# A fourth Strassen pair in the first half of the cross output projection, and a later place in the program for the loads of the transposed memory

## The chip, the cores and the metric

The kernel runs on one core of a Trainium2 chip. The metric is the device time of one execution in microseconds (us); lower is better. Three runs of the kernel before gave 2434.51, 2434.72 and 2436.06 us, a median of 2434.72 us.

## What is computed

One layer of a streaming encoder on 256 tokens of width 2048: a SwiGLU feed-forward block, a mixer of two attentions with gates, a cross attention on 256 memory tokens, and a second SwiGLU block, each followed by a residual and a LayerNorm. The change touches the cross attention:

```python
def memory_cross_attention(h, mem, mem_ln_g, mem_ln_b, w_xq, w_xkv, w_xo):
    m = layer_norm(mem, mem_ln_g, mem_ln_b)
    q = (h @ w_xq).reshape(b, s, X_HEADS, X_HEAD_DIM)          # 4 heads of 512
    kv = (m @ w_xkv).reshape(b, m_len, 2, X_HEADS, X_HEAD_DIM)
    k, v = kv[:, :, 0], kv[:, :, 1]
    sc = jnp.einsum('bqhd,bkhd->bhqk', q, k).astype(jnp.float32) / math.sqrt(X_HEAD_DIM)
    p = jax.nn.softmax(sc, axis=-1).astype(v.dtype)
    o = jnp.einsum('bhqk,bkhd->bqhd', p, v).reshape(b, s, D_MODEL)
    return o @ w_xo                                              # 256x2048 by 2048x2048
...
h = layer_norm(ALPHA * h + xa, ln_x_g, ln_x_b)
```

## The kernel before

**Precision.** Each float32 matrix is split into a high plane `hi` (a cast to fp32r on ScalarE, ACT, line 264 for weights and 255 for activations) and a low plane `lo` (source minus high plane on VectorE, DVE, lines 267 and 256). A product takes three matmuls: hi by hi, hi by lo, lo by hi. TensorE (PE) accumulates them in PSUM.

**Pairs.** The weights of a projection arrive in blocks of 128 x 2048 floats (1 MB, line 193, through three buffers `raw`). One block holds a pair of k-tiles by 1024 columns, and its number is `c`. `pair_group` takes the blocks in an order, by default 0, 1, 2 and so on. A plain pair (`mm_pair`, line 311) is 24 matmuls of 512 columns: two k-tiles, two halves of the tokens, two halves of the columns, three passes. A Strassen pair (`mm_sums`, line 366; the dictionary `at` says which pairs) needs 21, seven products by three passes. Four of the seven products go to four extra banks `qs`, which `shared` (lines 679 to 684) adds to the result once, behind the last such pair. For its 21 matmuls a Strassen pair needs sums of its weights (`weight_sums`, DVE, lines 248 and 250), high and low planes of 1536 columns of the block and of 2048 columns of sums where a plain pair has 2048 columns, and four forms of its activations (`sum_forms`, DVE, lines 321 and 325, then a cast on ACT and a subtraction on DVE, lines 255 and 256). In the cross output the staged sums lie in block T3 and their planes in T0 and T1, one buffer each.

**Cross output.** `cross` ends in `all_items`: `out_pair` computes the first 1024 output columns from eight pairs of `w_xo`, three of them (2, 4, 6) Strassen pairs; `out_proj` computes the other 1024 columns with plain matmuls (line 298) from `w_xo_r`, and its last part is woven with the LayerNorm of the first token half (`ln_scale`, `ln_T`: statistics at line 390, aggregation at 395, scaling at 413 and 415, transposes on PE at 421, planes at 428, 430, 255 and 256). Woven between the pairs are `out(2)` and `out(3)`, the products of probabilities and values for heads 2 and 3 (line 1543 before, 1545 after), and the forms. Heads 0 to 3 lie in H4, H5, X2, X3; pair `c` reads head `c // 2`. Behind comes the second feed-forward block, whose first weights (`ffn_gate`) are loaded while the LayerNorm runs.

**Memory.** `mem_norm` normalizes the memory tokens during the mixer's output projection (`w_out`). Its `load` (lines 1336 to 1342) sends the memory rows (`mem`, two loads into T1 and T2) and the transposed memory (`memT`, two loads into T3 and H4) on POOL's queue. It is woven in ahead of the first block of `w_out`. The mixer's last values are turned by DMA transposes on SP's queue (line 850) meanwhile.

**Order.** Each engine runs its instructions in the order in which the scheduler of the tile framework put them when the program was built; a wait holds whatever stands behind it on that engine. Buffers are given out by name, so a load waits until the last reader of its block is done.

Of the kernel before, what the change touches and what calls it, by code (L numbers as in the profile page):

```python
# [21 lines left out]
KT = D // P  # L22
# [12 lines left out]
AT_YB = (2, 4, 6), (4, 6)  # L35
SUMS_XQ = {4: ("H5", 0), 6: ("H5", 1), 2: None}
SUMS_XV = {4: ("T3", 0), 6: ("T3", 1), 2: None}
SUMS_XO = {2: None, 4: ("H2", 0), 6: ("H2", 1)}

AT_XQ = (4, 6), (2, 4, 6)  # L40
AT_XV = (2, 4, 6), (4, 6)
SUM_HOME = ("X2", "X3"),
# [59 lines left out]
class Kernel:  # L102
# [513 lines left out]
            turn = None  # L616
            f0 += nf

    def out_pair(self, bank, src, g, nk, x, at, fx, scale, st, sums_in=SUM_HOME):

        nc, h = self.nc, self.h
        ps, qs = {}, {}

        def shared():
            for (tt, a), s in qs["add"].items():
                c = (2 * g + a) * 512
                hs = h[tt][:, c:c + 512]
                if scale:
                    nc.vector.scalar_tensor_tensor(hs, hs, ALPHA, s, ALU.mult, ALU.add)
                else:  # L630
                    nc.vector.tensor_tensor(hs, hs, s, ALU.add)

        def finish():
            for tt in range(2):
                for a in range(2):
                    self.finish(tt, 2 * g + a, ps[tt, a], scale and not at, st)
        self.pair_group(bank, src, 512, nk, x, at, fx, ps, qs, shared, sums_in)
        self.add(finish)

    def group_tile(self, j):  # L640
# [690 lines left out]
    def mem_norm(self):  # L1331

        nc, t = self.nc, self.t
        e = self.mem = {}

        def load():
            e["m"] = [self.block(f"T{1 + tt}", (P, D)) for tt in range(2)]
            e["raw"] = [self.block(g) for g in ("T3", "H4")]
            for j in range(2):
                nc.gpsimd.dma_start(e["m"][j], t["mem"][j])  # L1340
            for j in range(2):
                nc.gpsimd.dma_start(e["raw"][j], t["memT"][:, 8 * j:8 * j + 8, :])

        def stat(tt):
            def fn():
                if tt == 0:
                    e["diag"] = self.w2((P, 4, P))
                    e["ones"] = self.w1((P, P))
                    nc.gpsimd.memset(e["ones"], 1.0)
                st = self.ln_begin()  # L1350
                with self.tc.issue_after(self.last_lo.ins):
                    for n in range(4):
                        self.ln_piece(st, e["m"][tt], n)
                kept = self.chain
                mean, r, _ = self.ln_scale(st)
                self.chain = kept
                for k, v in enumerate((mean, r)):
                    nc.vector.tensor_scalar(e["diag"][:, 2 * k + tt, :], self.ident, v, None, ALU.mult)
                if tt:
                    e["mT"] = self.act(["H0", "H1", "H2", "H3"])  # L1360
            return fn

        def spread():

            ps = self.at_tile()
            with self.tc.issue_after(self.last_mm.ins):
                for j in range(4):
                    nc.tensor.matmul(ps[:, j * P:(j + 1) * P], e["ones"], e["diag"][:, j, :], start=True, stop=True)
            e["mr"] = self.w2((P, 2, 1, S))
            nc.scalar.copy(e["mr"].rearrange("p a o s -> p (a o s)"), ps)  # L1370

        def quarter(q):
            def fn():
                v = e["raw"][q // 2][:, q % 2 * 4:q % 2 * 4 + 4, :]
                for k, op in enumerate((ALU.subtract, ALU.mult)):
                    nc.vector.tensor_tensor(v, v, e["mr"][:, k].to_broadcast([P, 4, S]), op)
                for j in range(4):
                    kt = 4 * q + j
                    nc.scalar.activation(v[:, j, :], v[:, j, :], AF.Identity,
                                         bias=self.vec("mem_ln_b", kt), scale=self.vec("mem_ln_g", kt))  # L1380
                self.split(v, e["mT"].blk(0, 4 * q, 4), e["mT"].blk(1, 4 * q, 4))
            return fn

        return {0: [load], 4: [stat(0)], 7: [stat(1)], 9: [spread], 10: [quarter(0)], 11: [quarter(1)], 13: [quarter(2)], 14: [quarter(3)]}

    def turned_norm(self, ln, st, x):

# [45 lines left out]
    def cross(self, xT, st, norm, steps_out):  # L1433
        nc, t, e = self.nc, self.t, self.mem
        q, k, v, sc, pt, o, turned = {}, {}, {}, {}, {}, {}, {}
        fq, fv, fx = {}, {}, {}
        m, x = lambda: e["mT"], lambda: o["t"]
# [96 lines left out]
        def out(h):  # L1534
            def fn():
                if h == 0:
                    o["t"] = Act([])
                o["t"].blocks += self.act([HEADS[h]]).blocks
                for j in range(4):
                    ps = self.mm_tile() if h > 1 else self.at_tile()  # L1540
                    for kt in range(2):
                        for i, (a, b) in enumerate(PASSES):
                            nc.tensor.matmul(ps[:, :S], v[h][:, a, kt, j * P:(j + 1) * P],
                                             pt[h][b][:, kt * S:(kt + 1) * S],
                                             start=(kt + i == 0), stop=(kt == 1 and i == 2))
                    self.split(ps[:, :S], o["t"].at(0, 4 * h + j), o["t"].at(1, 4 * h + j))
            return fn

        form_q = lambda c: self.forms_step(fq, SUMS_XQ, c, xT)
        form_v = lambda c: self.forms_step(fv, SUMS_XV, c, m)  # L1550
        form = lambda c: self.forms_step(fx, SUMS_XO, c, x)
        gb = lambda i: lambda: self.gb_apply(1, self.h, (i,))
# [13 lines left out]
        scale, planes, nsend, njoin = norm  # L1566
# [11 lines left out]
                    7: [join(3)]}, 1)  # L1578

        def all_items():  # L1580
            self.out_pair(1, t["w_xo"][0], 0, KT, x, SUMS_XO, fx, True, st, (("T0", "T1"), "T3"))
            self.out_proj("w_xo_r", KT, x, True, st, steps_out, (
                ("T0", "T1", "early"), ("T2", "T3", "early"), ("H0", "H1", "early"), ("H2", "H3", "early")), 2)
        self.weave(self.collect(all_items), {1: [out(2), out(3), form(2)], 2: [form(4)], 4: [form(6)]}, prio=0)

    def final_steps(self, st):
        nc, t, h = self.nc, self.t, self.h
# [83 lines left out]
def _tok(w):  # L1671

    k, n = w.shape
    return w.reshape(k // P, P, n // 512, 512).transpose(2, 1, 0, 3).reshape(n // 512, P, k // P * 512)


def _pairs(u, g, n, turned):


    import numpy as np  # L1680
    k, c = u.shape
    w = np.stack([m.reshape(k // P, P, c // n, n) for m in (u, g)])
    for j in range(c // n):
        for i in turned[j]:
            w[:, 2 * i:2 * i + 2, :, j] = w[::-1, 2 * i:2 * i + 2, :, j].copy()
    return w.transpose(3, 2, 1, 0, 4).reshape(c // n, P, k // P * 2 * n)


def _halves(w):

    w = w.reshape(w.shape[0], -1, 2, 512)
    return [w[:, :, i].reshape(w.shape[0], -1) for i in (0, 1)]
# [6 lines left out]
def _layout(i):  # L1699
# [45 lines left out]
    w = a["w_xo"][0]  # L1745
    r["w_xo"] = _pairs(*_halves(w[:, :D // 2]), 512, [SUMS_XO])
    r["w_xo_r"] = _tok(w[:, D // 2:])
# [29 lines left out]
```

## Time and profile before

| | |
|---|---|
| median of three runs | 2434.72 us |
| profiled execution | 2432.88 us, of which its span 2431.0 us |
| PE busy | 2422.4 us, 11280 matmuls |
| DVE busy | 2131.3 us |
| ACT busy | 1553.1 us |
| POOL busy | 36.0 us |
| DMA | 516.21 MB, mean 212 GB/s |
| cross output, first half (`w_xo`) | from 1649.68 to 1697.34 us in the span |

Times in the profile are microseconds from the start of the span. Busy time is the share in which an engine had at least one instruction in flight. A matmul's busy time (about 390 ns for 512 columns) overlaps its neighbours', so a rate is read from the starts of rows that follow each other. The same holds for DVE and ACT, where an instruction starts some 90 ns before the one ahead of it ends. A row of the timeline merges equal instructions (xcount); a bracket at its end tells the idle time before it and what ended it.

### The profile page before, as it was taken

The page shows a single profiled execution, that of the slowest core. Times are in us where ns is not written, and L with a number is a line of the kernel's source. Part 1 is how long each engine was busy: PE and PEld are TensorE (multiplying, and loading weights), DVE is VectorE, ACT ScalarE, POOL GpSimd, SP SyncE. Part 2 cuts the span into 40 slices and gives each one's busy share as a digit, 9 for nine tenths or more (in the row PEclk, how much of TensorE's full clock was granted, in tenths as well). Part 3 has the DMA queues.
Part 4 walks back from the last instruction along what each step waited for, and adds up shares of the span by engine and source line. Part 5 has one row for each costly group of instructions (what it writes and reads, how often), then busy time and mean ns, then how long its engine had stood idle before and what let it go on. Part 6 is the DMA issues. An engine that isn't in the chain of part 4 may idle for free.

```text
span 2431.0 us, 29704 instructions
## 1 busy us (share of the span) xinstructions
PE 2422.4 (100%) x11280; PEld 2021.5 (83%) x11280; DVE 2131.3 (88%) x2437; ACT 1553.1 (64%) x2022; POOL 36.0 (1%) x81
## 2 busy tenths in 40 slices
PE   9999999999999999999999999999999999999999
PEld 8888888889888888888888888888888888888887
DVE  8999989899889998789788889879879999888997
ACT  6676745666555557878565787755666675556662
POOL 0000000000000001000000000000000000000000
PEclk9999999999999999999999999999999999999999
DMA  7766656667645657776577577655556766666665
GB/s 267 253 211 215 206 201 223 210 202 230 218 174 211 216 202 242 236 203 176 186 254 246 170 237 214 216 183 192 191 199 213 228 222 211 219 207 207 201 222 180
DMA packets 176416, 516.21 MB, mean 212 GB/s; under 512 B 111729, under 2 KB 112497, under 8 KB 121105
## 3 DMA queue, kind: packets, MB, share of 16 engines
q1 hardware_dynamic: 170816, 495.83, 61.5%
q0 software_dynamic: 4592, 17.30, 2.3%
q8 instruction: 88, 1.44, 0.2%
q10 hardware_dynamic: 864, 1.18, 0.1%
q14 instruction: 56, 0.45, 0.1%
HBM read 485.30 MB, written 2.10 MB: 200 GB/s over the span
## 4 chain that ended last, share of the span: by engine, by line
PE 89%; DVE 4%; ACT 3%; DMA 2%; issue 1%; SPq 0%; DVEq 0%; ACTq 0%
PE at L311 25%; PE mm L311 24%; PE at L366 11%; PE mm L366 11%; PE mm L298 10%; PE mm L277 4%; PE mm L279 2%; DVE lo L267 2%; ACT hi L264 2%; PE at L1034 1%; DMA raw<-w_xq 1%; DMA raw<-w_xk 0%; DMA raw<-w_xv 0%; PE at L1088 0%; ACT w L832 0%
## 5 line engine op out<-in xcount | busy, mean ns | idle before, releaser
L264 ACT CAST hi<-raw 128x1024 fp32r<-128x1024 f32 (+1 forms) x852 | 803.4, 980 | 440.4 <-PE at L311 130.5
L267 DVE TENSOR_TENSOR lo<-raw,hi 128x2048 fp32r<-128x2048 f32 (+1 forms) x427 | 902.2, 2115 | 136.1 <-ACT hi L264 129.1
L311 PE MATMUL mm<-hi,T 128*128 128x512 f32 (+1 forms) x1312 | 308.1, 384 | 0.5 <-ACT hi L255 0.4
L264 ACT CAST X<-H 128x1024 fp32r<-128x1024 f32 (+1 forms) x170 | 174.7, 1034 | 171.5 <-DVE H L248 117.5
L311 PEld LDWEIGHTS mm<-hi,T 128*128 128x128 f32 x1312 | 244.4, 188 | 46.8 <-ACT hi L255 0.9
L311 PE MATMUL at<-hi,T 128*128 128x512 f32 x1136 | 272.3, 390 | 0.0
L311 PEld LDWEIGHTS at<-hi,T 128*128 128x128 f32 x1136 | 213.3, 188 | 44.4
L267 DVE TENSOR_TENSOR X<-H,X 128x2048 fp32r<-128x2048 f32 (+1 forms) x85 | 191.5, 2253 | 62.1 <-ACT X L264 61.9
L311 PE MATMUL mm<-lo,T 128*128 128x512 f32 (+1 forms) x656 | 158.1, 383 | 0.0
L311 PE MATMUL at<-lo,T 128*128 128x512 f32 x568 | 141.0, 390 | 0.0
L311 PEld LDWEIGHTS mm<-lo,T 128*128 128x128 f32 x656 | 122.2, 188 | 22.4
L311 PE MATMUL at<-hi,H 128*128 128x512 f32 x560 | 133.4, 390 | 0.0
L311 PEld LDWEIGHTS at<-lo,T 128*128 128x128 f32 x568 | 106.7, 188 | 22.1
L311 PEld LDWEIGHTS at<-hi,H 128*128 128x128 f32 x560 | 105.0, 188 | 21.5
L250 DVE TENSOR_TENSOR H<-H,raw 128x512 f32<-128x512 f32 (+1 forms) x170 | 115.7, 681 | 2.4
L311 PE MATMUL mm<-hi,H 128*128 128x512 f32 x480 | 115.6, 392 | 0.4 <-DVE w L684 0.4
L311 PEld LDWEIGHTS mm<-hi,H 128*128 128x128 f32 x480 | 89.6, 188 | 19.5 <-DVE w L684 0.8
L248 DVE TENSOR_TENSOR H<-raw 128x1024 f32<-128x1024 f32 (+1 forms) x85 | 102.2, 1203 | 0.5 <-DMA raw<-w_gate 0.3
L366 PE MATMUL mm<-X,X 128*128 128x512 f32 x342 | 91.3, 392 | 0.0
L264 ACT CAST X<-raw 128x1024 fp32r<-128x1024 f32 (+1 forms) x54 | 55.4, 1035 | 48.7 <-DVE raw L250 38.7
L366 PE MATMUL at<-X,X 128*128 128x512 f32 (+1 forms) x315 | 82.7, 386 | 0.0
L854 ACT COPY w<-w 128x1024 uint16<-128x1024 uint16 (+1 forms) x60 | 75.6, 1273 | 1.5 <-DMA w<-w 1.4
(387 smaller groups left out, 4153.9 us busy)
## 6 DMA issues: line engine op xcount, KB each, us to landing
raw<-ffn_w_in SPq DMA_DIRECT2D x150, 1024.0 KB, 4.9
raw<-ffn_w_out SPq DMA_DIRECT2D x66, 1024.0 KB, 4.9
raw<-w_gate SPq DMA_DIRECT2D x32, 1024.0 KB, 4.7
raw<-ffn_w_out_r SPq DMA_DIRECT2D x16, 1024.0 KB, 5.0
raw<-w_qk SPq DMA_DIRECT2D x16, 1024.0 KB, 5.3
raw<-w_o_b SPq DMA_DIRECT2D x16, 1024.0 KB, 4.8
raw<-w_out SPq DMA_DIRECT2D x16, 1024.0 KB, 5.1
raw<-w_xk SPq DMA_DIRECT2D x16, 1024.0 KB, 5.3
```

The source lines that it names most:

```text
L248: self.nc.vector.tensor_tensor(two[0], two[1], raw[:, :m].unsqueeze(1).to_broadcast([P, 2, m]), ALU.add)
L250: self.nc.vector.tensor_tensor(t[:, a * m:a * m + m], t[:, b * m:b * m + m], raw[:, a * m:a * m + m], ALU.add)
L264: self.last_hi = self.nc.scalar.copy(hi[:, c:d], src[:, c:d])
L267: self.last_lo = self.nc.vector.tensor_tensor(lo[:, :n], src, hi[:, :n].bitcast(F32), ALU.subtract)
L277: self.nc.tensor.matmul(ps, hi[j], x.both(kt), start=(j == 0), stop=False)
L279: self.last_mm = self.nc.tensor.matmul(ps[:, :S], lo[j], x.at(0, kt), start=False, stop=(j == n - 1))
L298: self.last_mm = self.nc.tensor.matmul(ps, x.at(xi, kt)[:, tt * P:(tt + 1) * P], w[wi][:, j * 512 + c:j * 512 + c + m], start=(start and j ...
L311: self.last_mm = self.nc.tensor.matmul(ps[tt, g][:, :n], x.at(xi, kt)[:, tt * P:(tt + 1) * P], w[wi][:, c:c + n], start=first and j + wi + ...
L366: self.last_mm = self.nc.tensor.matmul(bank[:, :m], a[xi], v[wi][:, c * m:(c + 1) * m], start=own and first and wi + xi == 0, stop=own and ...
L854: self.nc.scalar.copy(self.words(u, n).rearrange("p (c k) -> p k c", k=2), self.words(s, n).rearrange("p (k c) -> p k c", k=2))
L1034: nc.tensor.matmul(ps[:, c0:c0 + nk], q[:, tt * P:(tt + 1) * P], k[:, :nk], start=(j == 0), stop=(j == len(parts) - 1))
```

## The change

Pair 0 joins pairs 2, 4 and 6 as a Strassen pair; its forms go to block F. The eight blocks are taken in the order 1, 0, 3, 2, 4, 5, 6, 7. A form step for pair 0 is woven in ahead of the first block. In `mem_norm`, the allocation of the two buffers for the transposed memory and its two loads move to an item of their own, five blocks of `w_out` later. The host lays the blocks of `w_xo` out by the same dictionary.

```diff
-SUMS_XO = {2: None, 4: ("H2", 0), 6: ("H2", 1)}
+SUMS_XO, ORDER_XO = {2: None, 4: ("H2", 0), 6: ("H2", 1), 0: ("F", 0)}, (1, 0, 3, 2, 4, 5, 6, 7)
...
-    def out_pair(self, bank, src, g, nk, x, at, fx, scale, st, sums_in=SUM_HOME):
+    def out_pair(self, bank, src, g, nk, x, at, fx, scale, st, sums_in=SUM_HOME, order=None):
...
-        self.pair_group(bank, src, 512, nk, x, at, fx, ps, qs, shared, sums_in)
+        self.pair_group(bank, src, 512, nk, x, at, fx, ps, qs, shared, sums_in, order)
...
             e["m"] = [self.block(f"T{1 + tt}", (P, D)) for tt in range(2)]
-            e["raw"] = [self.block(g) for g in ("T3", "H4")]
             for j in range(2):
                 nc.gpsimd.dma_start(e["m"][j], t["mem"][j])
+
+        def load_turned():
+            e["raw"] = [self.block(g) for g in ("T3", "H4")]
             for j in range(2):
                 nc.gpsimd.dma_start(e["raw"][j], t["memT"][:, 8 * j:8 * j + 8, :])
...
-        return {0: [load], 4: [stat(0)], 7: [stat(1)], 9: [spread], 10: [quarter(0)], 11: [quarter(1)], 13: [quarter(2)], 14: [quarter(3)]}
+        return {0: [load], 4: [stat(0)], 5: [load_turned], 7: [stat(1)], 9: [spread], 10: [quarter(0)], 11: [quarter(1)], 13: [quarter(2)], 14: [quarter(3)]}
...
-            self.out_pair(1, t["w_xo"][0], 0, KT, x, SUMS_XO, fx, True, st, (("T0", "T1"), "T3"))
+            self.out_pair(1, t["w_xo"][0], 0, KT, x, SUMS_XO, fx, True, st, (("T0", "T1"), "T3"), ORDER_XO)
...
-        self.weave(self.collect(all_items), {1: [out(2), out(3), form(2)], 2: [form(4)], 4: [form(6)]}, prio=0)
+        self.weave(self.collect(all_items), {0: [form(0)], 1: [out(2), out(3), form(2)], 2: [form(4)], 4: [form(6)]}, prio=0)
```

How the built programs differ: up to the middle of the last block of `w_xv` the two programs have the same instructions in the same order on every engine. On POOL and SP the order is the same throughout, and the loads of `mem` and `memT` on POOL wait for the same semaphores at the same counts. From there on PE, DVE and ACT differ at the cross output.

PE just behind `out(2)`, before: the second plain block (pair 1, `hi_13311`) follows, with `out(3)` (`X_2056`) in its gaps.

```order
L1543 MATMUL mm_13402<-X_2039_13209,T_2055_13322 128x256 x6
L311 MATMUL at_13336<-hi_13311,H_1973_12758 128x512 x2
L311 MATMUL at_13337<-hi_13311,H_1973_12758 128x512 x2
L311 MATMUL at_13338<-hi_13311,H_1973_12758 128x512 x2
L311 MATMUL at_13339<-hi_13311,H_1973_12758 128x512 x2
L311 MATMUL at_13336<-hi_13311,H_1973_12758 128x512 x2
L1543 MATMUL mm_13412<-X_2039_13209,X_2056_13329 128x256 x6
```

PE at the same place with the change. `hi_13315` and `lo_13316` are the planes of pair 0's block, T_2054 (T0) and T_2055 (T1) those of its sums, `hi_13379` and `lo_13380` those of the plain pair 3, F_13339 the forms of pair 0. Between `out(2)` and the first of these rows stand seven matmuls: three on pair 0's own planes and four on `hi_13379`.

```order
L366 MATMUL at_13351<-T_2054_13320,H_1973_12758 128x512 x2
L311 MATMUL at_13349<-hi_13379,H_2000_12939 128x512 x2
L311 MATMUL at_13352<-hi_13379,H_2000_12939 128x512 x2
L311 MATMUL at_13349<-lo_13380,H_2000_12939 128x512
L311 MATMUL at_13352<-lo_13380,H_2000_12939 128x512
L311 MATMUL at_13349<-lo_13380,H_2000_12939 128x512
L311 MATMUL at_13352<-lo_13380,H_2000_12939 128x512
L366 MATMUL at_13351<-T_2055_13321,H_1973_12758 128x512
L311 MATMUL at_13351<-hi_13379,H_2000_12939 128x512 x4
L311 MATMUL at_13351<-lo_13380,H_2000_12939 128x512 x2
L366 MATMUL at_13350<-hi_13315,F_13339 128x512
```

Pair 0's products, placed behind `out(2)`, are spread among the plain products of pair 3; between the last matmul of `out(2)` and the first that reads T_2055 stand 17 matmuls of 512 columns, and 7 more (itself and six on pair 3) from there to the first that reads F.

DVE at that place with the change: `raw_13272` is the block of pair 0, T_2047 (T3) its sums, `raw_13377` the block of pair 3, X_2057 the values for `out(3)`.

```order
L250 TENSOR_TENSOR T_2047_13274<-T_2047_13274,raw_13272 128x512
L267 TENSOR_TENSOR lo_13316<-raw_13272,hi_13315 128x1536
L256 TENSOR_TENSOR X_2057_13332<-w_2051_13284,X_2057_13332 128x512
L250 TENSOR_TENSOR T_2047_13274<-T_2047_13274,raw_13272 128x512
L321 TENSOR_TENSOR w_2059_13340<-H_1973_12758 128x512
L267 TENSOR_TENSOR lo_13380<-raw_13377,hi_13379 128x2048
L267 TENSOR_TENSOR T_2055_13321<-T_2047_13274,T_2054_13320 128x2048
L325 TENSOR_TENSOR w_2060_13341<-w_2059_13340 128x128 x2
L325 TENSOR_TENSOR w_2060_13341<-w_2060_13341,w_2059_13340 128x128
L248 TENSOR_TENSOR T_2069_13386<-raw_13384 128x1024
L325 TENSOR_TENSOR w_2060_13341<-w_2059_13340,w_2060_13341 128x128
```

The sums of pair 0 (line 248) were started behind line 682; their last part, their low planes and the low planes of pair 3 stand behind the planes for `out(3)`; the form of pair 0 (lines 321 and 325) is shared out around them, and its cast on ACT follows the last row.

DVE in the norm of the first token half (`h_101`), before: one subtraction of weight planes (`X_2152`) stands between the last piece of `h_101` (line 752) and the scale of its norm.

```order
L267 TENSOR_TENSOR lo_13894<-raw_13891,hi_13893 128x2048
L752 SCALAR_TENSOR_TENSOR h_101<-h_101,mm_13898 128x512
L390 BN_STATS bn_13731<-h_101 128x6
L267 TENSOR_TENSOR X_2152_13914<-raw_13911,X_2151_13913 128x2048
L395 BN_AGGR mv_13956<-bn_13731 128x2
L400 TENSOR_SCALAR v_13957<-mv_13956 128x1
```

DVE there with the change:

```order
L267 TENSOR_TENSOR lo_13875<-raw_13872,hi_13874 128x2048
L752 SCALAR_TENSOR_TENSOR h_101<-h_101,mm_13914 128x512
L267 TENSOR_TENSOR lo_13910<-raw_13907,hi_13909 128x2048
L390 BN_STATS bn_13747<-h_101 128x6
L395 BN_AGGR mv_13972<-bn_13747 128x2
L267 TENSOR_TENSOR X_2158_13930<-raw_13927,X_2157_13929 128x2048
L400 TENSOR_SCALAR v_13973<-mv_13972 128x1
```

The subtraction for the second block of `ffn_gate` (`lo_13894`, now `lo_13910`) moved from ahead of line 752 to behind it, so two of them now stand in the chain of the norm.

## Rows read from the trace of the kernel before

**Rows 1.** The page: span and busy time of the engines.
```profile
span 2431.0 us, 29704 instructions
...
PE 2422.4 (100%) x11280; PEld 2021.5 (83%) x11280; DVE 2131.3 (88%) x2437; ACT 1553.1 (64%) x2022; POOL 36.0 (1%) x81
```
**Rows 2.** Waits of PE, whole span: total us, times, longest; the first of eight.
```profile
PE at L493 <- DVE w L470: 1.1, 1, 1.1
```
**Rows 3.** Windows: us, busy us of engines, granted clock, DMA share, GB/s.
```profile
1644.20:1697.30 53.10, 53.10 (x256) 44.38 (x256) 52.14 (x69) 31.91 (x47) 0.00 (x0) 1.00 0.56 191
1697.30:1712.20 14.90, 14.90 (x67) 12.34 (x66) 14.86 (x15) 6.33 (x7) 0.00 (x0) 1.00 0.50 181
1712.20:1738.10 25.90, 25.90 (x116) 21.42 (x115) 20.21 (x24) 15.16 (x16) 0.00 (x0) 1.00 0.85 310
```
**Rows 4.** Timeline of PE: start us, us, engine, line, operation, tiles, shape, count.
```profile
1649.68 3.79 PE L311 MATMUL at<-hi,H 128*128 128x512 f32 x16
...
1655.12 3.04 PE L1543 MATMUL mm<-X,T 128*128 128x256 f32 x24
1657.99 2.46 PE L311 MATMUL at<-hi,H 128*128 128x512 f32 x10
...
1695.52 1.98 PE L311 MATMUL at<-lo,X 128*128 128x512 f32 x8
...
1729.98 5.60 PE L298 MATMUL mm<-T,H 128*128 128x512 f32 x24
...
1738.14 1.03 PE L421 MATMUL at<-ident,h 128*128 128x128 f32 x8
```
**Rows 5.** Timeline of DVE, first part of the cross output.
```profile
1647.52 0.68 DVE L682 TENSOR_TENSOR w<-w,w 128x512 f32<-128x512 f32 x1
...
1655.84 0.69 DVE L256 TENSOR_TENSOR X<-w,X 128x512 fp32r<-128x512 f32 x1
1656.44 1.23 DVE L248 TENSOR_TENSOR T<-raw 128x1024 f32<-128x1024 f32 x1
1657.57 1.76 DVE L267 TENSOR_TENSOR lo<-raw,hi 128x1536 fp32r<-128x1536 f32 x1
1659.24 0.69 DVE L250 TENSOR_TENSOR T<-T,raw 128x512 f32<-128x512 f32 x1
...
1661.98 2.29 DVE L267 TENSOR_TENSOR T<-T,T 128x2048 fp32r<-128x2048 f32 x1
1664.19 1.41 DVE L256 TENSOR_TENSOR X<-mm,X 128x256 fp32r<-128x256 f32 x4
1665.52 0.68 DVE L321 TENSOR_TENSOR w<-H 128x512 f32<-128x512 f32 x1
...
1667.25 0.49 DVE L325 TENSOR_TENSOR w<-w 128x128 f32<-128x128 f32 x2
```
**Rows 6.** Timeline of DVE, planes of pairs 6 and 7.
```profile
1689.15 4.49 DVE L267 TENSOR_TENSOR lo<-raw,hi 128x2048 fp32r<-128x2048 f32 x2
```
**Rows 7.** Timeline of ACT: a cast of 512 columns, then two of 1024.
```profile
1685.14 0.62 ACT L255 CAST H<-w 128x512 fp32r<-128x512 f32 x1
1685.66 2.00 ACT L264 CAST hi<-raw 128x1024 fp32r<-128x1024 f32 x2
```
**Rows 8.** Timeline of DVE, norm of the first token half.
```profile
1730.91 0.68 DVE L752 SCALAR_TENSOR_TENSOR h<-h,mm 128x512 f32<-128x512 f32 x1
...
1732.23 2.27 DVE L267 TENSOR_TENSOR X<-raw,X 128x2048 fp32r<-128x2048 f32 x1
1734.42 0.26 DVE L395 BATCH_NORM_AGGREGATE mv<-bn 128x2 f32<-128x24 f32 x1
...
1736.84 1.00 DVE L413 TENSOR_SCALAR h<-h,mv,y 128x512 f32<-128x512 f32 x2
```
**Rows 9.** Timeline of ACT, first casts of the second feed-forward block.
```profile
1726.66 2.00 ACT L264 CAST hi<-raw 128x1024 fp32r<-128x1024 f32 x2 [2.99 <-DMA raw<-ffn_gate]
```
**Rows 10.** The window of the mixer's transposes and the memory loads (columns as in Rows 3).
```profile
1249.00:1275.00 26.00, 26.00 (x117) 21.53 (x116) 22.96 (x18) 20.83 (x24) 1.60 (x3) 1.00 1.03 336
```

## The prediction

> **What bounds the kernel now.** I read the page first. PE is busy for 2422.4 of 2431.0 us of the span [rows 1]: all its idle time together is 8.6 us, and the longest single wait for another engine is 1.1 us [rows 2]. So time is gained here only by fewer matmuls, and a stall that the change opens on PE comes on top whole. The windows come next. In the stretch around the first half of the cross output PE is busy for 53.10 of 53.10 us at a granted clock of 1.00, the upper of the two levels (2.4 GHz), so the clock gives nothing back. DVE is busy for 52.14 of the same 53.10 us, then 14.86 of 14.90; only behind 1712 us does it have room, 20.21 of 25.90 [rows 3]. DVE is the second full engine, and the change gives work from the first to it. ACT has room (31.91 of 53.10).
>
> **What the change removes.** A plain pair of 24 matmuls runs from 1649.68 to 1655.12 us, 5.44 us, or 0.2267 us for each [rows 4]. Pair 0 now takes 21: 3 x 0.2267 = **0.68 us less on PE**. The Trainium skill, "TensorE: Matmul & The Clock Gate", section "Back-to-back issue gap", gives about 131 ns for a matmul of 512 columns in a stream of weight loads and matmuls; by it the saving would be 0.39 us and the sum below +5.7. The trace does not agree with it here, with 226.7 ns over a whole pair.
>
> **What it adds on DVE.** Prices are from start to start; an instruction ends 0.10 us behind the start of the next (1656.44 + 1.23 = 1657.67 against 1657.57) [rows 5], so a result counts 0.1 us later for another engine. 512 columns take 0.60 us, 1024 take 1.13, 1536 take 1.67, 2048 take 2.21 (1661.98 to 1664.19), and 128 take 0.20 ((0.49 - 0.09) / 2); 256 take 0.33 ((1.41 - 0.09) / 4) [rows 5]. The sums of pair 0's weights: 1.13 + 2 x 0.60 = 2.33. Its forms: 0.60 + 4 x 0.20 + 0.60 = 2.0. Its planes: 1.67 + 2.21 in place of 2.21, so 1.67. Together **6.0 us**, into a stretch where DVE has 0.96 us free. ACT gets one cast of 1024 and two of 512 more, 0.95 ((2.00 - 0.10) / 2) and 0.52 each [rows 7], 2.0 us, for which it has room. Six more microseconds behind PE cannot all be hidden; the question is where PE meets them. By the order of the instructions that is at three places.
>
> **Place 1, pair 0 itself.** DVE starts line 682 at 1647.52 and is free of it at 1648.12 [rows 5]. From there to the end of T_2055, the low planes of pair 0's sums, DVE's order holds: line 248, 1.13; lines 683, 684 and three of line 1495, 3.0; three of line 256, 1.8; one more of line 1495, 0.6; two of line 250, one of 256 and one of 321, 2.4; planes of 1536 columns, 1.67; two planes of 2048, 4.4. That is 15.0 us: done at 1663.1, seen by PE at 1663.2. PE ends `out(2)` at 1657.99 as before [rows 4], since nothing on its way there has changed, and 17 matmuls later, at 1657.99 + 3.85 = 1661.84, it wants T_2055: **a wait of 1.4 us**. Seven matmuls on, at 1663.2 + 1.6 = 1664.8, it wants F, the forms of pair 0. On DVE those end three instructions of 128, one of 1024 and one of 128 after 1663.1, at 1665.05; the cast on ACT of 0.62 us, busy [rows 7], makes it 1665.7 to 1665.8: **1.0 us** more. Between, `out(3)` cannot fill the gap, because a wait holds what stands behind it on PE. Sum 2.4 us; bounds: 0 if DVE's list were 2.4 us shorter than I read it, 3 if ACT's casts are held as well.
>
> **Between.** Pairs 2 and 4 then meet their sums and planes with DVE late: small waits, 0.3 us (none up to 0.8; eight waits of 0.2 to 1.1 us are what PE shows anywhere [rows 2]).
>
> **Place 2, pairs 6 and 7.** From 1665.05 DVE has to run, up to the sums of pair 6: three planes of 2048, two of 1536, two of 1024, nine of 512, eight of 256 and twelve of 128, together 6.6 + 3.3 + 2.3 + 5.4 + 2.7 + 2.4 = 22.7 us, to 1687.7. Behind that ACT casts the first half of T0 (0.95) and the first half of pair 7's high plane (0.95) [rows 7], so the latter stands at about 1689.9 with the hand-overs. PE has 91 matmuls of 512 columns and 24 of 256 from 1665.8: 20.63 + 2.72 = 23.35 us, so it wants that plane at 1689.15: 0.7 us. Two matmuls later it wants the second half of T0, another 0.5 to 0.7. **1.4 us**; none if ACT takes its casts in a luckier moment. As a bound from the other side, by DVE's queue alone: pair 7's low planes were done at 1691.35 (half of 4.4 from 1689.15) [rows 6], 6.0 later is 1697.35, or 1696.4 with the free 0.96 used; PE wants them at 1695.52 - 0.68 = 1694.84 [rows 4] if it never waited. So the stage cannot cost less than 1.6 us of waits, and more wherever DVE has to wait as well.
>
> **Place 3, the norm of the first half.** Behind the first half DVE has free time [rows 3], and its lag is worked off. But the subtraction for the second `ffn_gate` block now stands inside the chain of the norm. From PE's last matmul for `h_101` the chain is: hand-over 0.2, line 752 0.6, a plane 2.2, statistics 0.6, aggregation 0.3 (1734.42 on), a plane 2.2 (1732.23 to 1734.42), the small operations 2.1 (to 1736.84), line 413 0.5, hand-over 0.1 [rows 8]: 8.8 to 9.0 us. PE has 36 plain matmuls, 8.16 us, from 1729.98 to the transposes at 1738.14 before [rows 4], and 38 with the change, 8.6: a wait of 0.2 to 0.4 with every block at hand. They will hardly be: ACT waited 2.99 us for this very block, until 1726.66 [rows 9], in a stretch where the DMA engines run at 0.85 and 310 GB/s [rows 3]. Before, two casts and DVE were done with it just as PE got to 1729.98; a lag in the release of buffers goes into these loads, and a load later by 1 to 2 us now lands in the chain. I take 1.5 (0.2 to 2.4). Then the low plane of the first transposed tile stands behind line 752 of `h_102`, which starts when PE's last product is done and takes 0.6 us: 0.5 more (to 0.6). **2.0 us.**
>
> **The moved loads.** On POOL the loads of `mem` and `memT` stand in the same order, behind the same counts; and from 1249 to 1275 us, around them, PE is busy for 26.00 of 26.00 us although the DMA engines are full at 1.03 [rows 10]. Nothing: 0 us, and no gain could show.
>
> **Sum.** -0.68 + 2.4 + 0.3 + 1.4 + 2.0 = **+5.4 us**. The profiled execution took 2432.88 us, 1.84 below the median of 2434.72; on it the sum gives 2438.3, on the median **2440.1 us**. A change under 0.2%, 4.9 us, can hardly be told from none, so this stands just beyond that line. With the low bounds of the stage (1.6) and of the norm (0.7) it is +1.6, with the high ones (3, 0.8, 1.4, 3.0) +7.5.
>
> **Rivals.** (a) *The lag stays in the cross output.* The loads of `ffn_gate` are not late, the norm costs 0.4 or nothing, or place 2 falls away: +3.4 +- 1.3, about 2438.1. For it speaks DVE's free time behind 1712 us, 5.7 us of 25.9 [rows 3]; against it, two planes in the chain whatever the loads do. Within 0.2%. (b) *The other side: nothing stalls.* PE keeps only its 0.68 us less: 2434.0. That needs DVE's list at place 1 to end by 1661.8, 1.4 us sooner than I count, and the forms 2.4 sooner, so line 248 and the planes would have to run before PE wants them; it decides itself there, for a wait at place 1 is already more than the gain. Against it: DVE was full for 52.14 of 53.10 us. (c) *The moved loads do something*: if the transposes or PE's stage around 1260 us changed, up to the 8.6 us that PE idles could come back; but it waits nowhere near, and the order is the same. (d) *The lag grows*: `ffn_gate`'s blocks come 3 us late or more, the second half of the norm is held as well, and the second feed-forward block starts late: +8 to +10, about 2443.5. For it speaks DMA at 0.85 there; against it, that DVE and ACT regain their lead from 1712 us.
>
> **How the numbers follow.** The forecast has 0.50, of which 0.42 beyond 0.2% (its own range is 2438.5 to 2441.8). (a) has 0.31, of which 0.03 runs beyond 0.2%; (b) 0.05; (c) 0.02; (d) 0.12. Faster by over 0.2% would need almost 5 of the 8.6 idle microseconds back, which is (c) alone: 0.02. Slower is 0.42 + 0.03 + 0.12 = 0.57. Within 0.2% is 0.08 + 0.28 + 0.05 = 0.41. The range leaves out (b), (c) and most of (d), about 0.17: it goes from the low bounds, +1.6 or 2436.3, to 2442.6, a little above the high ones (+7.5 or 2442.2) for a part of (d).
>
> **What would show it.** Right: the page's span about 5 us longer with 3 matmuls fewer; PE's waits gain a wait of line 366 for T of line 267 near 1662 us, one for F of line 255 near 1664.8, one or two for casts of line 264 near 1689, and one of line 421 for line 413 near 1741; DVE's window from 1644 to the end of the first half is full. Wrong: no wait of line 366 at 1662 us (then the count of DVE's list is wrong); no wait at line 421 (then rival (a)); a different start of the `memT` loads (c); waits in the second feed-forward block that stood not there before (d).

## The result and the profile after

22 runs of each kernel gave medians of 2434.17 us before and 2438.72 us with the change: **4.55 us slower**, a ratio of 1.0019 with a 95% interval of 1.0013 to 1.0025 (3.2 to 6.1 us). 2440.1 us was forecast, 5.4 us slower, within 2436.3 to 2442.6. The loss is real, and at 0.19% it stands just within the line that the forecast drew at 0.2%: beyond that line the forecast had put 0.57, within it 0.41. Of the 1.4 us between 2440.1 and 2438.72, 0.55 is the median before, which three runs had put at 2434.72.

The profiled execution took 2440.40 us. Its page, to be set against [rows 1], has three matmuls fewer and 7.6 us more of span.

```profile
span 2438.6 us, 29710 instructions
...
PE 2425.1 (99%) x11277; PEld 2019.1 (83%) x11277; DVE 2136.8 (88%) x2447; ACT 1554.3 (64%) x2025; POOL 35.8 (1%) x81
```

7.6 us is more than the runs differ by. The first plain block of the cross output starts at 1652.85 us here and at 1649.68 before [rows 4]: 3.17 us were lost ahead of it, in instructions that both programs share; 1.2 of them are one wait of PE at line 421, at 681 us. The kernel of experiment 2, which has no fourth pair, starts that block at 1652.40. So spans of single executions vary by 3 us in code that nobody changed, and a change of 4 us is read from its own stretch. From the first plain block's first matmul to the first `mm<-lo,T` of `ffn_gate` it is 94.80 us before (1649.68 to 1744.48) and 98.97 us after (1652.85 to 1751.82): **+4.17 us**. "The stretch" below is always this one, in one profiled execution of each kernel. Its last row before, and its first and last row after:

```profile
1744.48 1.08 PE L298 MATMUL mm<-lo,T 128*128 128x512 f32 x4
```

```profile
1652.85 3.79 PE L311 MATMUL at<-hi,H 128*128 128x512 f32 x16
...
1751.82 0.39 PE L298 MATMUL mm<-lo,T 128*128 128x512 f32 x1
```

Behind it, from 1744.48 and from 1751.82 to the spans' ends, 0.3 us differ.

The windows of the same three parts as in [rows 3] (us, busy us of PE, PEld, DVE, ACT and POOL, granted clock, DMA share, GB/s):

```profile
1647.40:1703.60 56.20, 53.83 (x253) 43.08 (x252) 55.62 (x75) 33.56 (x49) 0.00 (x0) 1.00 0.46 162
1703.60:1718.50 14.90, 14.90 (x67) 12.33 (x67) 14.90 (x18) 6.36 (x7) 0.00 (x0) 1.00 0.52 179
1718.50:1744.40 25.90, 25.90 (x116) 21.46 (x115) 21.39 (x23) 14.02 (x14) 0.00 (x0) 1.00 0.87 321
```

DVE is now full (55.62 of 56.20 us), and PE is not: it idles 2.37 us. The granted clock stays at 1.00. Of PE's waits in the whole span (engine and line, what it waited for, total us, times, longest; [rows 2] has those before), these lie in the stretch:

```profile
PE at L366 <- DVE T L267: 0.9, 1, 0.9
...
PE at L366 <- ACT F L255: 0.7, 1, 0.7
PE at L311 <- ACT hi L264: 0.5, 1, 0.5
...
PE mm L298 <- DVE T L256: 0.3, 1, 0.3
PE at L421 <- DVE h L413: 0.2, 1, 0.2
...
PE at L366 <- ACT T L264: 0.2, 1, 0.2
```

These six are new, each at a place that the forecast named. They add up to 2.8 us, while the stretch grew by 4.17 and by 4.85 without the three matmuls. The timeline of PE shows why (start us, us, engine, line, operation, tiles, shape, count, idle time before):

```profile
1661.17 0.63 PE L366 MATMUL at<-hi,H 128*128 128x512 f32 x2
...
1664.25 1.07 PE L311 MATMUL at<-lo,H 128*128 128x512 f32 x4
1666.24 0.50 PE L366 MATMUL at<-T,H 128*128 128x512 f32 x1 [0.93 <-DVE T L267]
1666.58 1.09 PE L311 MATMUL at<-hi,H 128*128 128x512 f32 x4
1667.50 0.63 PE L311 MATMUL at<-lo,H 128*128 128x512 f32 x2
1668.84 0.49 PE L366 MATMUL at<-hi,F 128*128 128x512 f32 x1 [0.70 <-ACT F L255]
...
1693.66 0.73 PE L311 MATMUL at<-hi,X 128*128 128x512 f32 x2 [0.53 <-ACT hi L264]
1694.60 0.73 PE L366 MATMUL at<-T,X 128*128 128x512 f32 x2 [0.21 <-ACT T L264]
```

Four matmuls from 1664.25 end their turn at 1665.16, but the next starts at 1666.24: 1.08 us late, where the bracket says 0.93, because it counts from the modelled end of the last one. And the matmul behind it comes 0.34 us later instead of 0.23. So a wait costs about 0.25 us more than its bracket. Counted from start to start against 0.2267 us, PE lost 4.85 us more than before: 2.1 at pair 0, 0.3 between, 1.4 at pairs 6 and 7, 1.0 in the norm (each rounded).

The norm, DVE's timeline, for [rows 8]:

```profile
1736.50 0.69 DVE L752 SCALAR_TENSOR_TENSOR h<-h,mm 128x512 f32<-128x512 f32 x1 [0.77 <-PE mm L298]
1737.33 2.29 DVE L267 TENSOR_TENSOR lo<-raw,hi 128x2048 fp32r<-128x2048 f32 x1
1739.54 0.69 DVE L390 BATCH_NORM_STATS2 bn<-h 128x6 f32<-128x512 f32 x1
...
1740.44 2.23 DVE L267 TENSOR_TENSOR X<-raw,X 128x2048 fp32r<-128x2048 f32 x1
```

ACT's cast of the block that the plane of 1737.33 belongs to, for [rows 9]:

```profile
1735.29 2.00 ACT L264 CAST hi<-raw 128x1024 fp32r<-128x1024 f32 x2 [1.89 <-DMA raw<-ffn_gate]
```

And PE around it, for the end of [rows 4]:

```profile
1736.30 5.60 PE L298 MATMUL mm<-T,H 128*128 128x512 f32 x24
1741.74 3.33 PE L298 MATMUL mm<-H,X 128*128 128x512 f32 x14
1745.30 1.09 PE L421 MATMUL at<-ident,h 128*128 128x128 f32 x8 [0.23 <-DVE h L413]
...
1750.09 1.89 PE L298 MATMUL mm<-hi,T 128*128 128x512 f32 x7 [0.28 <-DVE T L256]
```

Two planes stand in the chain, and the transposes start 1745.30 - 1736.30 - 38 x 0.2267 = 0.39 us late. The block's cast ends at 1737.29, 0.99 us behind PE's 1736.30; before it ended 1.32 us ahead of it (1728.66 against 1729.98 in [rows 4, 9]). It comes 2.3 us later, but about when line 752 is done: the plane starts 0.83 us behind the start of that line, where 0.60 is usual.

### The profile page after: what moved, and what is told of

It is laid out like the page before. It is cut to its first block, busy times and chain, and to the rows that moved or that the text cites. A ratio compares the mean times of both kernels' runs of the same rounds, so it can differ in the third digit from the quotient of the medians.

```text
span 2438.6 us, 29710 instructions
## 1 busy us (share of the span) xinstructions
PE 2425.1 (99%) x11277; PEld 2019.1 (83%) x11277; DVE 2136.8 (88%) x2447; ACT 1554.3 (64%) x2025; POOL 35.8 (1%) x81
## 4 chain that ended last, share of the span: by engine, by line
PE 83%; DVE 7%; ACT 4%; DMA 3%; issue 2%; SPq 0%; ACTq 0%; DVEq 0%
PE at L311 24%; PE mm L311 22%; PE at L366 11%; PE mm L366 10%; PE mm L298 9%; PE mm L277 3%; DVE lo L267 3%; ACT hi L264 2%; PE mm L279 1%; DMA raw<-w_xv 1%; PE at L1034 1%; DMA raw<-w_xq 1%; DMA raw<-w_xk 0%; ACT w L832 0%; DVE T L256 0%
```

## The experiments

The theory: the whole loss is PE waiting for the 6.0 us that pair 0 adds to a full DVE, paid at pair 0, at pairs 6 and 7 and in the norm. The rivals: the other order of the blocks costs; the fourth pair costs by itself; the moved loads do something.

| kernel | added to DVE in the cross output, us | stretch, us | ratio to before (95%) |
|---|---|---|---|
| before | 0 | 94.80 | 1 |
| 1 loads moved alone | 0 | 94.72 | 1.0003 (0.9995 to 1.0012) |
| 2 order alone | 0 | 94.43 | 1.0001 (0.9992 to 1.0010) |
| 3 no sums, no forms | 1.7 | 94.77 | 1.0006 (0.9997 to 1.0015) |
| 6 both forms early, other order | 2.0 | 94.85 | 0.9999 (0.9990 to 1.0007) |
| 10 no sums | 3.7 | 96.51 | one run |
| 11 no forms | 4.0 | 96.36 | one run |
| 5 form of pair 0 early | 4.0 | 97.78 | 1.0012 (1.0004 to 1.0021) |
| the change | 6.0 | 98.97 | 1.0019 (1.0013 to 1.0025) |
| 4 sums twice | 8.3 | 101.07 | 1.0035 (1.0023 to 1.0048) |

Each edit is shown against the changed kernel, without the lines that only hand a value on. DVE's added work is summed from the prices of the forecast. The three kernels with the three pairs of before read 94.43 to 94.80 us, which tells how far single executions of the stretch differ. All but the first three rows have PE's three matmuls fewer.

**1. The moved loads alone.**

```diff
-SUMS_XO, ORDER_XO = {2: None, 4: ("H2", 0), 6: ("H2", 1), 0: ("F", 0)}, (1, 0, 3, 2, 4, 5, 6, 7)
+SUMS_XO, ORDER_XO = {2: None, 4: ("H2", 0), 6: ("H2", 1)}, None
...
-        self.weave(self.collect(all_items), {0: [form(0)], 1: [out(2), out(3), form(2)], 2: [form(4)], 4: [form(6)]}, prio=0)
+        self.weave(self.collect(all_items), {1: [out(2), out(3), form(2)], 2: [form(4)], 4: [form(6)]}, prio=0)
```

> The kernel before with nothing but the loads of the transposed memory moved. My theory (all of the loss is PE waiting for DVE's added work in the cross output and for the norm behind it): 0 us against the kernel before, ratio 0.9995 to 1.0005, and the first memT load in the same place between the same neighbours. Rival, the moved loads cost or give something: a ratio off 1 by 0.0008 or more (2 us).

1.0003, and a stretch of 94.72 us. In the trace each of the five engines has the same instructions in the same order as in the kernel before. This part of the change is nothing.

**2. The order alone.** The edit of 1, but with the order (1, 0, 3, 2, 4, 5, 6, 7).

> Three Strassen pairs as before, with the eight blocks of the first half taken as 1, 0, 3, 2, 4, 5, 6, 7. My theory: DVE has no work more, so 0 us (-0.7 to +0.7), no wait of PE of 0.4 us or more between 1650 and 1750 us, and one plane (not two) between line 752 and line 413 in the norm. Rival, the order of the blocks is what costs (its loads, its banks): +2 us or more, with waits of PE at pairs 3 to 7.

1.0001; the stretch is 94.43 us, no wait of PE of 0.4 us or more stands in it, and the chain of the norm has one plane. The order costs nothing.

**3. The fourth pair without its sums and forms.** `zero` is true for pair 0 alone; experiments 4, 8 and 10 use it too.

```diff
-                sums[i] = self.weight_sums(raw, queue[i].m, self.block(home, (P, 2048)) if home else self.raw_tile())
+                sums[i] = raw if queue[i].zero else self.weight_sums(raw, queue[i].m, self.block(home, (P, 2048)) if home else self.raw_tile())
...
-            self.sum_forms(x(), 2 * c, out)
+            self.sum_forms(x(), 2 * c, out) if not (e is not None and homes is SUMS_XO and c == 0) else e.update({0: [[x().at(a, k)[:, t * P:(t + 1) * P] for a in (0, 1)] for k in (0, 1) for t in (0, 1)]})
```

> The changed kernel without the DVE work that pair 0 adds ahead of its planes: its weight sums are not formed (the planes of the sums are made from the block itself) and its activations' forms are not formed (plain parts of the heads stand in). PE keeps the 21 matmuls, DVE's added work falls from 6.0 to 1.7 us. My theory: the waits at T of line 267 and F of line 255 (2.3 us together) and those at pairs 6 and 7 (1.3 us) go, the norm keeps up to 1 us: -0.7 to +1.0 us against the kernel before. Rival, the fourth pair costs by itself whatever DVE does (PE's order, the banks, the loads): +3.5 us or more, as in the changed kernel.

The waits at pair 0 and at pairs 6 and 7 are gone. What is left is 0.4 us at line 421; the stretch is as before, 94.77 us. The ratio, 1.0006, cannot be told from none. The fourth pair by itself costs nothing that can be seen, nor does its saving of 0.68 us show.

**4. The sums of pair 0 twice.**

```diff
-                sums[i] = self.weight_sums(raw, queue[i].m, self.block(home, (P, 2048)) if home else self.raw_tile())
+                sums[i] = self.weight_sums(raw, queue[i].m, self.block(home, (P, 2048)) if home else self.raw_tile()); queue[i].zero and self.weight_sums(raw, queue[i].m, sums[i])
```

> The changed kernel with the weight sums of pair 0 formed twice into the same block: 2.3 us more on DVE, nothing else. My theory (DVE is full from there to the end of the first half): PE pays nearly all of it, +2 us on the changed kernel, +6 to +7 us against the kernel before, and PE's wait for a plane of T in pair 0 grows from 0.9 to about 3 us. Rival, DVE has room and the waits are of another making: +4.5 us as in the changed kernel, give or take 0.7.

1.0035, or 8.5 us, with an interval of 5.6 to 11.7 that takes in the 6 to 7 expected; the stretch is 101.07 us, 6.3 more than before and 2.10 more than with the change, for 2.33 of DVE. That PE pays was right. The place was not: PE's waits at pair 0 and at the pairs behind are spread over other tiles.

```profile
PE at L366 <- ACT T L264: 2.7, 3, 1.4
...
PE at L366 <- DVE T L267: 1.0, 1, 1.0
PE at L311 <- DVE lo L267: 0.7, 1, 0.7
```

The first matmul on T0 now waits for ACT's cast of the later sums, and T1, behind it on PE, has then only 1.0 us left to wait.

**5. The form of pair 0 in `w_xv`.**

```diff
-        group(val, {1: [out(1), ready(3), scores(2)], 3: [send(2), scores(3), gb(3)], 5: [join(2), send(3)],
+        group(val, {1: [out(1), ready(3), scores(2)], 3: [send(2), scores(3), gb(3)], 5: [join(2), send(3), form(0)],
...
-        self.weave(self.collect(all_items), {0: [form(0)], 1: [out(2), out(3), form(2)], 2: [form(4)], 4: [form(6)]}, prio=0)
+        self.weave(self.collect(all_items), {1: [out(2), out(3), form(2)], 2: [form(4)], 4: [form(6)]}, prio=0)
```

> The changed kernel with the forms of pair 0 (2.0 us of DVE, head 0 is ready long before) made during the second half of w_xv, where DVE is busy for about 15 of 20 us. My theory: in the cross output DVE's added work falls from 6.0 to 4.0 us; PE's wait for F (0.9 us) goes, the wait for T in pair 0 shrinks or goes, later waits and the norm stay: from the first plain pair to the ninth product of ffn_gate 97 to 98 us against 94.8 before and 99.0 changed, +2 to +3.2 us in the time. Rival, the waits only follow from where pair 0 stands and not from DVE's sum: everything but the wait for F stays, 98.1 us.

97.78 us, +2.6 us in the time. Both waits of pair 0 are gone, and a new one of 1.25 us stands at pair 4, for ACT's cast of T: what one place no longer pays, the next one does.

**6. Both early forms, and the pair later.** The edit of 5 for forms 0 and 2 (at steps 3 and 5 of `w_xv`), and

```diff
-SUMS_XO, ORDER_XO = {2: None, 4: ("H2", 0), 6: ("H2", 1), 0: ("F", 0)}, (1, 0, 3, 2, 4, 5, 6, 7)
+SUMS_XO, ORDER_XO = {2: ("F", 1), 4: ("H2", 0), 6: ("H2", 1), 0: ("F", 0)}, (1, 3, 0, 2, 4, 5, 6, 7)
```

> The changed kernel with the forms of pairs 0 and 2 (4.0 us of DVE) made during w_xv and the blocks taken as 1, 3, 0, 2, 4, 5, 6, 7, so that the planes of pair 0's sums are wanted 5.4 us later. My theory: DVE's work in the cross output grows by 2 us in place of 6, where it had 1 us free; no wait of PE of 0.3 us in the first half, the norm keeps 0 to 1 us: the stretch 94.0 to 95.1 us against 94.8 before, -0.8 to +0.3 us in the time, which the runs can't tell from none. Rival, four Strassen pairs are more than the stage holds wherever their forms are made: waits of 2 us or more, +1.5 us or more.

0.9999 and 94.85 us: the loss is gone with the pair in place. How much of this the forms give and how much the later place was not tried apart. Its window over the first half has PE busy throughout beside a DVE that is almost as full as with the change:

```profile
1644.00:1697.00 53.00, 53.00 (x258) 44.82 (x257) 52.72 (x63) 32.72 (x45) 0.00 (x0) 1.00 0.53 182
```

The norm takes back the 0.68 us: its two waits are 0.5 us each.

**7. The norm in the order of the kernel before.** On top of 6, line 752 of `h_101` behind the low plane of the second `ffn_gate` block:

```diff
-            with self.prio(SOON if n == 3 and st is not None else 0):
+            with self.prio(SOON if n == 3 and st is not None else 0), self.tc.issue_after(self.los[-2].ins) if wname == "w_xo_r" and n == 3 and tt == 0 else nullcontext():
```

> The kernel of the run before in this call, with line 752 of h_101 put behind the low plane of the second ffn_gate block, which is the order of the kernel before. My theory (two planes in the chain of the norm are what PE waits for at line 421): the waits at line 421 (0.4 us) and at the first product of ffn_gate (0.5 us) go, the stretch is 0.5 to 1.0 us shorter than in the run before. Rival, the chain is held by the load of that block, which is late, and the order only follows from it: no shorter, up to 1 us longer.

The theory failed, and the rival holds: 95.41 us, 0.56 longer than 6. DVE now sits idle for that plane and only then takes line 752:

```profile
1730.68 2.29 DVE L267 TENSOR_TENSOR lo<-raw,hi 128x2048 fp32r<-128x2048 f32 x1 [1.61 <-ACT hi L264]
1732.89 0.68 DVE L752 SCALAR_TENSOR_TENSOR h<-h,mm 128x512 f32<-128x512 f32 x1
```

The block is late; the order of the two makes the best of it.

**8. The sums of pair 0 on POOL.** `weight_sums` gets an engine, and pair 0 passes POOL's:

```diff
-                sums[i] = self.weight_sums(raw, queue[i].m, self.block(home, (P, 2048)) if home else self.raw_tile())
+                sums[i] = self.weight_sums(raw, queue[i].m, self.block(home, (P, 2048)) if home else self.raw_tile(), self.nc.gpsimd if queue[i].zero else None)
```

> The changed kernel with the weight sums of pair 0 formed on POOL, which stands idle there (one of its additions of 512 columns takes 1.26 us in the kernel before, so some 5.1 us for 2.3 us of DVE's). My theory: DVE's added work falls to 3.7 us and the stretch to 96.5 to 97.5 us against 94.8 before and 99.0 changed. Rival, POOL and DVE hold each other up while both read two operands: DVE's instructions beside it grow by more than 2.3 us in sum, and the stretch is 99 us or longer.

1.0041 (1.0028 to 1.0053), with a stretch of 104.36 us in place of the 96.5 to 97.5 of the theory. Three things came together. POOL, then DVE:

```profile
1646.37 4.21 POOL L248 TENSOR_TENSOR T<-raw 128x1024 f32<-128x1024 f32 x1 [47.52 <-DMA raw<-w_xo]
1650.66 2.96 POOL L250 TENSOR_TENSOR T<-T,raw 128x512 f32<-128x512 f32 x2
```

```profile
1646.04 2.29 DVE L267 TENSOR_TENSOR lo<-raw,hi 128x2048 fp32r<-128x2048 f32 x1 [0.17 <-ACT hi L264]
1648.25 2.88 DVE L682 TENSOR_TENSOR w<-w,w 128x512 f32<-128x512 f32 x1
1654.74 2.29 DVE L267 TENSOR_TENSOR T<-T,T 128x2048 fp32r<-128x2048 f32 x1 [3.60 <-ACT T L264]
1656.95 0.68 DVE L683 TENSOR_TENSOR w<-w,at 128x512 f32<-128x512 f32 x1
```

Line 682 took 2.88 us for its usual 0.68 [rows 5]: it ends at 1651.13, 0.55 behind the end of POOL's addition at 1650.58. The rival was right in that. The larger part is an order: DVE now has the low planes of T ahead of line 683 and waits 3.60 us for POOL's sums, and PE waits 5.72 us for the result of line 684. The third thing stands in the last section. What POOL would be worth with line 683 ahead was not tried.

**9. The plane first.** On top of 6, line 752 of `h_102` behind the low planes of two transposed tiles:

```diff
+            with self.prio(SOON if n == 3 and st is not None else 0), self.tc.issue_after(self.ln_los["ln_x", 0, 1].ins) if wname == "w_xo_r" and n == 3 and tt == 1 else nullcontext():
```

> The kernel with both forms early and the order 1, 3, 0, 2, with line 752 of h_102 put behind the low planes of the first two transposed tiles on DVE. My theory (the second wait of the norm, 0.5 us at the first product of ffn_gate, is only that plane standing behind line 752): that wait goes, the stretch is 94.2 to 94.5 us against 94.85 without this edit and 94.8 in the kernel before; in the time -0.3 to -0.7 us, which the runs can't tell from none. Rival, the plane is late because of ACT's casts or of the transposes: the stretch stays at 94.7 to 95.0 us.

94.15 us: the second wait is gone, as PE's timeline shows. The products of `ffn_gate` follow the transposes at once.

```profile
1739.61 1.09 PE L421 MATMUL at<-ident,h 128*128 128x128 f32 x8 [0.17 <-DVE h L413]
1740.46 2.55 PE L298 MATMUL mm<-H,X 128*128 128x512 f32 x10
1742.85 1.04 PE L421 MATMUL at<-ident,h 128*128 128x128 f32 x8
1743.65 2.07 PE L298 MATMUL mm<-hi,T 128*128 128x512 f32 x8
```

Its stretch is 0.65 us shorter than that of the kernel before, about what the three matmuls take. In the time this cannot be seen: 1.0000 (0.9991 to 1.0009).

**10 and 11. No sums, and no forms.** One half each of the edit of 3.

> The changed kernel without the weight sums of pair 0 alone (the planes of the sums are made from the block itself): DVE's added work 3.7 us. My theory, PE pays for DVE's sum beyond 1 us: the stretch 96.0 to 97.5 us (94.8 before, 99.0 changed), no wait in pair 0, those at pairs 6 and 7 stay. Rival, the waits belong to pair 0's place: as changed but for the wait at T, 97.8 us.

96.51 us; pair 0 has no wait, pairs 6 and 7 keep theirs (0.67 and 0.38 us late).

> The changed kernel without the forms of pair 0 alone (plain parts of the heads stand in): DVE's added work 4.0 us, now not moved elsewhere but gone. My theory: the stretch 96.0 to 97.8 us, near that of the kernel whose forms are made early. Rival, the forms cost PE only their own wait at F: 98.0 us.

96.36 us, against 97.78 with the same 2.0 us made early. Part of the early form's saving was lost: in 5 the order has a longer wait at pair 4 (1.4 us late against 0.9) and the second wait of the norm, which 11 has not. The sum alone does not fix the loss to better than 1.4 us.

Three of the six waits name a cast of ACT, and the change gives work to ACT too. But 10, the change and 4 have the same casts on ACT and differ by 2.33 us on DVE each time: 96.51, 98.97 and 101.07 us. So these casts are late because of DVE's additions.

## Why the forecast was right, and where it was off

| step | forecast, us | measured in the stretch, us |
|---|---|---|
| three matmuls fewer | -0.68 | -0.68 |
| place 1, pair 0 | +2.4 | +2.1 |
| between | +0.3 | +0.3 |
| place 2, pairs 6 and 7 | +1.4 | +1.4 |
| place 3, the norm | +2.0 | +1.0 |
| the moved loads | 0 | 0 |
| sum | +5.4 | +4.2 |

- **What bounds.** PE was full and DVE nearly so; the change gave 0.68 us to the one and took 6.0 from the other. The series from 1.7 to 8.3 us of added DVE work runs from 94.77 to 101.07 us, 0.95 us of PE's time for each. That is shown for the cross output, for single versions within 1.4 us; the norm's share has another cause (place 3).
- **Place 1.** DVE's list of 15.0 us was right to the tenth: line 682 starts at 1650.49, and the start of the next instruction behind T_2055 is 1666.10, which is 0.60 + 15.0 us. PE came 1.2 us too early to T (1.4 forecast) and 1.0 us too early to F (1.0 forecast). Some 0.2 us of waits around `out(3)` that the kernel before had there went.
- **Place 2.** 0.7 and 0.4 us at the two tiles named, and 0.3 on the matmuls behind them.
- **Place 3 failed by a factor of two.** The step was "I take 1.5 (0.2 to 2.4)": a lag in the release of buffers was to bring a `ffn_gate` block 1 to 2 us late, and that was to land in the chain. The block did come 2.3 us later, but by the order of the program and not by a lag. The first `ffn_gate` load starts when DVE is done with a plane of T. Before, that plane stands ahead of a line 752; with the change it stands behind it, and that line waits for PE. DVE and SP before:

```profile
1714.54 2.29 DVE L267 TENSOR_TENSOR T<-raw,T 128x2048 fp32r<-128x2048 f32 x1 [2.37 <-ACT T L264]
1716.75 0.68 DVE L752 SCALAR_TENSOR_TENSOR h<-h,mm 128x512 f32<-128x512 f32 x1
```

```profile
1716.86 9.49 SPq L193 DMA_DIRECT2D raw<-ffn_gate  x4
```

and with the change:

```profile
1722.90 0.69 DVE L752 SCALAR_TENSOR_TENSOR h<-h,mm 128x512 f32<-128x512 f32 x1 [2.13 <-PE mm L298]
...
1724.23 2.27 DVE L267 TENSOR_TENSOR T<-raw,T 128x2048 fp32r<-128x2048 f32 x1
```

```profile
1726.53 9.55 SPq L193 DMA_DIRECT2D raw<-ffn_gate  x4
```

So the first load starts 13.1 us ahead of PE's row of 1729.98 before, and 9.8 us ahead of the same row, at 1736.30, with the change. All ten kernels with the fourth pair have this order and 9.8 us, whether 1.7 or 8.3 us were added to DVE; experiments 1 and 2 have the order of before, and 13.1 and 13.2 us. The delay then cost little, because the hand-over and line 752 have to run first in any case; they hid all but 0.2 us of it. The measured 0.39 is the high end of the "0.2 to 0.4 with every block at hand". The half microsecond behind line 752 of `h_102` was right; experiment 9 takes it away by order alone. So the norm's 1.0 us does not come from DVE's sum: its two waits have brackets of 0.2 to 0.3 us each in experiments 4, 5, 6 and 10 and in the change, with 2.0 to 8.3 us added. No run put the plane of T back ahead of line 752, so the order is read from the rows and not tried by itself.

- **The moved loads.** Nothing moved in the program; experiment 1 shows it.
- **The rivals.** (a) stood at 2438.1, and the measured 2438.72 lies between it and the forecast. Its condition, that the loads of `ffn_gate` are not late, did not hold; its 0.4 us or nothing for the norm was 1.0. (b), no stall, is what experiment 9 reaches with other edits. (c) and (d) did not come.

## What to carry to other kernels

Where two engines are full, price a trade between them by the second engine's own list, instruction by instruction, up to the place where the first wants each result: that gave each wait of the cross output to within 0.3 us. Compare the order of the two programs ahead of the next stage's loads as well: a plane that had moved behind an instruction waiting for PE made all loads of that stage start later, whatever work was added. Work that has its data long before (a form of a finished head) belongs into a stage in which that engine has room; with two such forms moved and the pair one place later the whole loss was gone, though which of the two did it is not shown. And read a change of some microseconds from its own stretch of the trace, since spans of single executions differ by 3 us in code that did not change.

## What was not expected of the hardware

- A wait costs PE about 0.25 us more than the bracket names: 0.93 was 1.08 from start to start, and the next matmul lost 0.11 more.
- After waits of up to 0.93 us with the change, and of 1.4 us in experiment 4, the granted clock stayed at 1.00, the upper level (2.4 GHz). After the 5.72 us of experiment 8 it was 0.50, the lower (1.2 GHz), and the next matmuls took 0.43 us each, which cost 1.9 us on top of the wait. PE there, then the windows of the wait and of the matmuls behind it:

```profile
1650.58 1.98 PE L311 MATMUL at<-hi,H 128*128 128x512 f32 x8
1658.28 3.78 PE L311 MATMUL at<-hi,H 128*128 128x512 f32 x8 [5.72 <-DVE w L684]
1661.86 2.10 PE L311 MATMUL at<-lo,H 128*128 128x512 f32 x8
```

```profile
1652.00:1658.00 6.00, 0.56 (x3) 0.13 (x1) 3.26 (x3) 2.51 (x3) 1.55 (x2) 0.77 0.07 27
1658.00:1660.00 2.00, 1.72 (x4) 1.43 (x5) 2.00 (x5) 1.09 (x2) 0.00 (x0) 0.50 0.02 4
...
1662.00:1664.00 2.00, 2.00 (x11) 1.67 (x10) 2.00 (x2) 1.86 (x2) 0.00 (x0) 0.98 0.00 0
```

- DVE's line 682 and POOL's addition did not run side by side: the one of 0.68 us took 2.88, and POOL's 4.21 us lie around the end of DVE's plane before it (1648.33) with 2.25 us behind that. The Trainium skill, "SBUF — State Buffer", section "SBUF: two separate sides", says that an instruction of VectorE with two inputs in SBUF and one of GpSimd that reads SBUF hold a shared pair of ports by a lock for their whole length, and the other waits. The trace agrees: line 682 ends 0.55 us behind the end of POOL's addition.
